# A 512-deep projection as seven block products instead of eight, in a hybrid streaming-encoder layer on one core

## The chip, the cores and the metric

The kernel runs on one core of a Trainium2 chip. The metric is the device time of one execution in microseconds (us). Five engines work from queues of their own: TensorE (PE, the matmuls), VectorE (DVE), ScalarE (ACT), GpSimd (POOL) and SyncE (SP, which only starts transfers). An instruction waits for the semaphores that it names, and what stands behind it on its engine waits with it.

## The reference, cut to what matters

One layer works on 1024 frames of 1024 features. Two mixers, a gated recurrence (`oa`) and a band attention (`ob`), each give 512 features for each frame; both are projected to 1024 features, gated and added, and the sum goes through the output projection. Then follow a SwiGLU and a gated embedding.

```python
h = rmsnorm(x, norm_mix_g[li])
z = h @ w_in[li]
qa, fa, ia, ga, qb, kb, vb, gate_a, gate_b = jnp.split(z, split_at, axis=-1)
oa = hgrn2_mixer(qa, fa, ia, ga, lower_bounds[li], hgrn_onorm_g[li])
ob = band_attention(qb, kb, vb, attn_qnorm_g[li], attn_knorm_g[li], attn_rel_bias[li])
merged = (jax.nn.sigmoid(gate_a) * (oa @ w_branch_a[li])
          + jax.nn.sigmoid(gate_b) * (ob @ w_branch_b[li]))
x = x + merged @ w_out[li]
h2 = rmsnorm(x, norm_ffn_g[li])
x = x + (jax.nn.silu(h2 @ w_ffn_gate[li]) * (h2 @ w_ffn_up[li])) @ w_ffn_down[li]
```

The change is about `ob @ w_branch_b` and what stands on both sides of it.

## The kernel before, in words

Everything is held with features on the 128 partitions and frames along the row. A float32 product is made of three matmuls on rounded operands: each operand is split into a rounded part (`hi`, written by ScalarE as a cast) and a residual (`lo`, source minus `hi`), and `gemm` (line 158) issues hi·hi, hi·lo, lo·hi. So every operand needs one cast on ScalarE and one subtraction on VectorE or GpSimd before TensorE can use it. Weights do the same: a unit of 128x1024 is loaded into one of two `raw` buffers, cast into `wh`, and its residual `wl` is written by GpSimd, or by VectorE and GpSimd by turns while `by_turns` is set (in the output projection). There are four buffers for `wh` and `wl` each. A raw buffer comes free when the residual is written, and the next load into it waits for that.

`order` (line 71) pins the order of the instructions on each engine as the program text issues them; VectorE, ScalarE and GpSimd calls through `self.V`, `self.A` and `self.G` are pinned too.

The stages that matter here, in order of time:

- The attention (`attention`, 32 steps of a pair of heads and 128 frames). `attn_pv` writes each result of 128 features by 128 frames to `ob[pair]`. The tiles of pairs 0 and 1 are stored to memory during the attention, those of 2 and 3 behind it, and all four are loaded again for the projection.
- The first branch (`branches`, first loop): 8 feature blocks by 2 halves of the frames, 12 matmuls of 128x512 each, the result times the gate into the tiles `m["B11"]` to `m["B22"]` (odd or even feature block, first or second half of the frames).
- The second branch (second loop): 8 by 2 results of 12 matmuls again, that is 192; VectorE multiplies each by its gate, and GpSimd (VectorE for the last four) adds it to the tile of `m`.
- The output projection (`out_proj`, through `passes`), a product of 2x2 blocks by the Winograd form of Strassen's method: seven products instead of eight, of sums of blocks of the weights and sums of blocks of `m`. Each pass is one product of 48 matmuls into four PSUM banks. The passes share three sets of banks; a later product adds onto an earlier one in the same bank. `added` adds each pass's banks into the residual stream `x`. The sums of `m` (T2, T3, T1, T4) are made by `branch_sums` on VectorE, for one half of the depth during the second branch and for the other at the start of the output projection, and `m_split` makes hi and lo of each operand. The sums of the weights (S1 to S4) are made in memory during the earlier stages by `dma_sums`: copies on SP's queue, then transfers with addition on POOL's queue.

In the text below, b: stands before a product of the second branch and o: before a pass of the output projection (o:A11 is the first one). Before the change the second branch has no such products.

Of the kernel before, what the change touches and what calls it, by code (L numbers as in the profile page):

```python
# [57 lines left out]
class Trunk:  # L58
# [334 lines left out]
    def hgrn_mix(self, h):  # L393
# [73 lines left out]
        for i in range(2):  # L467
# [4 lines left out]
            self.rest(False)  # L472
            yield 650
# [198 lines left out]
    def attn_pv(self, pair, b, pts, nb):  # L672
# [6 lines left out]
        self.last = self.A.copy(self.ob[pair][:, b * P:b * P + P], ps[:, :P])  # L679

    def attention(self):
# [41 lines left out]
        self.adds = chain(self.osum, self.wsum)  # L723
        for n in range(whole + 2):
# [4 lines left out]
            if n < whole:  # L729
                if steps[n][1] == 0:  # L730
                    self.ob.append(self.slot())
                scores(n, 0)
# [19 lines left out]
            if n == whole // 2 + 3:  # L752
                self.keep_heads(self.ob, self.obd, [0, 1])
# [234 lines left out]

    def branch_load(self, src):
# [7 lines left out]
    def branch_first(self):  # L997
        self.weights(0, ahead=3)
# [4 lines left out]
        for i, raw in enumerate(raws):  # L1003
            self.osrc.append(self.split(raw))
            yield
        self.keep_heads(self.ob, self.obd, [2, 3])
# [6 lines left out]
    def gate_load(self):  # L1013
        if len(self.bgates) < 2 * KC:
            for _ in range(2):
                t = self.slot(late=len(self.bgates) > 3)
                self.load(t, self.gd[len(self.bgates)])
                self.bgates.append(t)

    def branches(self):  # L1020
        nc, V = self.nc, self.V
        self.m = {}
        gates, load = self.bgates, self.gate_load
# [7 lines left out]
        src = self.osrc  # L1031
        for dd in range(4):
            (w,) = self.weights()
            next(self.adds, None)
            load()
            if dd == 1:
                raws = self.branch_load(self.obd)
                late = []
            for i in range(2):
                c = 2 * dd + i  # L1040
                for half in range(2):
                    hs = slice(half * HALF, half * HALF + HALF)
                    ps = yield from self.feature(w, src, half, off=i * HALF)
                    V.tensor_tensor(tile(c, half), ps, gates[c][:, hs], ALU.mult)
                    yield 2592
                if dd > 1:
                    late.append(self.split(raws[len(late)]))
        src = late
        for dd in range(4):
            (w,) = self.weights()  # L1050
            next(self.adds, None)
            load()
            for i in range(2):
                c = 2 * dd + i
                g = gates[KC + c]
                for half in range(2):
                    hs = slice(half * HALF, half * HALF + HALF)
                    ps = yield from self.feature(w, src, half, off=i * HALF)
                    V.tensor_tensor(g[:, hs], ps, g[:, hs], ALU.mult)
                    (self.G if dd < 3 else V).tensor_tensor(tile(c, half), tile(c, half), g[:, hs], ALU.add)  # L1060
                    yield 2592
            if dd == 1:
                self.branch_sums(0)
# [1141 lines left out]
```

## Time and profile before

| what | value |
|---|---|
| median of the runs | 1561.74 us (1558.86, 1561.74, 1562.02) |
| the profiled execution | 1560.97 us, its span 1559.2 us |
| granted TensorE clock, mean over the span | 0.999 |
| VectorE, ScalarE and GpSimd busy | 1126.4, 662.2 and 624.1 us |
| moved by transfers | 256.56 MB, mean 165 GB/s |

The span runs from the first to the last instruction; all positions below are microseconds from its start. A matmul's busy time overlaps the next one's, so TensorE's time in a stretch is read from the length of a stretch in which it does not wait, and not by adding up durations.

Stretches of the span, to find one's way: the attention ends at about 652, the first branch runs from there to 695.7, the second to 739.2, the output projection to about 817.

### The profile page before, as it was taken

How to read it: one execution, taken by the hardware profiler on the slowest of the kernel's cores; microseconds unless marked ns; L12 is line 12 of the kernel's file. 1: busy time of each engine (PE TensorE's matmuls, PEld its weight loads, DVE VectorE, ACT ScalarE, POOL GpSimd, SP SyncE). 2: the span in 40 equal slices, each digit the busy share in tenths (PEclk: the TensorE clock that was granted, in tenths of full speed). 3: DMA queues.
4: the chain of work that ended last, by engine and by line, in shares of the span. 5: the costliest groups of instructions: out<-in, count | busy, mean ns of one | idle time of the engine just before them, and what ended most of it. 6: DMA issues, size and time to landing. Idle time of an engine off the chain costs nothing.

```text
span 1559.2 us, 20881 instructions
## 1 busy us (share of the span) xinstructions
PE 1535.2 (98%) x7792; PEld 1281.2 (82%) x7792; DVE 1126.4 (72%) x1637; ACT 662.2 (42%) x1120; POOL 624.1 (40%) x349
## 2 busy tenths in 40 slices
PE   8999999999999999999999999999999999999998
PEld 6878888888888888788888888888888888888886
DVE  5777774676778778545988877777777766756667
ACT  6633333323367677521467322222222244446552
POOL 4243333010233222136211566665555545545546
PEclk9999999999999999999999999999999999999999
DMA  5453444887532343677344344443333288775325
GB/s 206 160 189 142 142 152 152 273 291 239 184 75 58 82 107 82 240 207 230 106 162 181 118 121 128 123 122 113 107 108 104 85 318 315 269 273 191 129 95 202
DMA packets 97094, 256.56 MB, mean 165 GB/s; under 512 B 10209, under 2 KB 14945, under 8 KB 96481
## 3 DMA queue, kind: packets, MB, share of 16 engines
q1 hardware_dynamic: 90448, 239.48, 44.1%
q0 software_dynamic: 6400, 15.73, 6.1%
q8 instruction: 61, 1.00, 0.3%
q14 instruction: 41, 0.33, 0.1%
q10 hardware_dynamic: 144, 0.02, 0.0%
HBM read 193.06 MB, written 93.59 MB: 184 GB/s over the span
## 4 chain that ended last, share of the span: by engine, by line
PE 91%; DVE 5%; DMA 2%; ACT 1%; issue 1%; SPq 0%; POOL 0%; DVEq 0%; ACTq 0%; POOLq 0%
PE pm L85 88%; DVE s L55 3%; PE pm L88 3%; DVE m L55 1%; DMA wr<-in_sz 0%; DVE q L55 0%; DMA wr<-in_su 0%; ACT m L55 0%; DMA s<-in_x 0%; DMA wr<-in_qk 0%; ACT wh L125 0%; SPq L80 0%; ACT s L55 0%; DVE s L227 0%; DVE wl L55 0%
## 5 line engine op out<-in xcount | busy, mean ns | idle before, releaser
L85 PE MATMUL pm<-s,whi 128*128 128x512 f32 x1792 | 551.7, 389 | 1.9 <-DVE t L55 1.9
L85 PE MATMUL pm<-s,wh 128*128 128x512 f32 (+1 forms) x1584 | 491.7, 391 | 7.5 <-ACT wh L125 5.0
L85 PEld LDWEIGHTS pm<-s,whi 128*128 128x128 f32 x1792 | 336.1, 188 | 72.3 <-DVE t L55 2.8
L85 PEld LDWEIGHTS pm<-s,wh 128*128 128x128 f32 x1584 | 295.3, 188 | 70.5 <-ACT wh L125 5.0
L85 PE MATMUL pm<-s,wlo 128*128 128x512 f32 x896 | 348.6, 389 | 0.0
L55 DVE TENSOR_TENSOR s<-s,s 128x512 f32<-128x512 f32 (+3 forms) x228 | 284.3, 1279 | 71.6 <-ACT s L55 42.7
L85 PE MATMUL pm<-s,wl 128*128 128x512 f32 x792 | 308.4, 389 | 0.5 <-POOL wl L133 0.5
L133 POOL TENSOR_TENSOR wl<-wr,wh 128x1024 fp32r<-128x1024 f32 (+2 forms) x72 | 175.6, 2443 | 220.5 <-ACT wh L125 207.2
L55 DVE TENSOR_TENSOR t<-pm,t 128x512 f32<-128x512 f32 x158 | 108.8, 689 | 128.9 <-PE pm L85 108.7
L85 PEld LDWEIGHTS pm<-s,wlo 128*128 128x128 f32 x896 | 168.2, 188 | 35.1
L125 ACT CAST wh<-wr 128x1024 fp32r<-128x1024 f32 (+2 forms) x106 | 106.5, 1005 | 208.9 <-PE pm L85 97.2
L85 PE MATMUL pm<-wh,s 128*128 128x512 f32 x512 | 179.9, 408 | 0.0
L85 PEld LDWEIGHTS pm<-s,wl 128*128 128x128 f32 x792 | 148.9, 188 | 31.9 <-POOL wl L133 1.2
L55 POOL TENSOR_TENSOR wlo<-wr,whi 128x512 fp32r<-128x512 f32 (+1 forms) x63 | 132.7, 2113 | 71.3 <-ACT whi L55 62.5
L55 POOL TENSOR_TENSOR wlo<-q,whi 128x512 fp32r<-128x512 f32 x62 | 97.2, 1568 | 139.7 <-ACT whi L55 110.6
L55 POOL TENSOR_TENSOR m<-m,mhalf 128x8 f32<-128x8 f32 (+1 forms) x24 | 35.0, 1458 | 241.3 <-DVE m L55 241.3
L55 ACT CAST whi<-q 128x512 fp32r<-128x512 f32 (+1 forms) x93 | 70.5, 759 | 110.6 <-PE pm L85 87.1
L55 ACT CAST s<-s 128x1024 fp32r<-128x1024 f32 (+1 forms) x94 | 90.4, 980 | 62.3 <-DVE s L55 31.8
L85 PEld LDWEIGHTS pm<-wh,s 128*128 128x128 f32 x512 | 96.9, 189 | 18.8
L55 POOL TENSOR_TENSOR s<-t,rb 128x512 f32<-128x512 f32 x44 | 70.7, 1608 | 99.3 <-ACT t L55 99.3
L85 PE MATMUL pm<-wl,s 128*128 128x512 f32 x256 | 100.5, 393 | 0.0
L55 ACT ACTIVATE t<-s 128x512 f32<-128x512 f32 x44 | 27.8, 632 | 158.3 <-DVE s L55 155.1
(145 smaller groups left out, 1850.0 us busy)
## 6 DMA issues: line engine op xcount, KB each, us to landing
s<-d SPq DMA_DIRECT2D x81, 512.0 KB, 6.3
d<-s SPq DMA_DIRECT2D x87, 256.0 KB, 2.3
wr<-d SPq DMA_DIRECT2D x36, 512.0 KB, 3.6
d<-s SPq DMA_DIRECT2D x32, 512.0 KB, 3.7
d<-t SPq DMA_DIRECT2D x46, 256.0 KB, 2.5
wr<-in_sg SPq DMA_DIRECT2D x22, 512.0 KB, 3.7
wr<-in_su SPq DMA_DIRECT2D x22, 512.0 KB, 4.1
s<-in_x SPq DMA_DIRECT2D x21, 512.0 KB, 8.2
```

The source lines that it names most:

```text
L55: return lambda *a, **k: self.trunk.order(op(*a, **k), self.key)
L85: return self.order(self.nc.tensor.matmul(*a, **k))
L88: return self.order(self.nc.tensor.transpose(*a, **k))
L125: self.nc.scalar.copy(hi[:, c], raw[:, c])
L133: rest.tensor_tensor(lo[:, c], raw[:, c], f32(hi[:, c]), ALU.subtract)
```

## The change

- The second branch becomes seven products of blocks. The attention's result is kept in SBUF in block layout: a tile for the odd or even pair of heads and each half of the frames (`ob[j, h]`, two pairs side by side). It is no longer stored and loaded again.
- `branch_ops` makes the sums and the hi and lo of these blocks on VectorE and ScalarE, partly during the first branch, partly during the second.
- The sums of the branch's weights are made by `dma_sums` in memory, as those of the output projection were: four copies and four adding transfers more. The adding transfers for the feed-forward weights come later in turn, eight more of them in the gate and up stage.
- `branch` runs the products kind by kind in the order A11, A12, S2, S1, S3, S4, A22, each 24 matmuls into four banks. After A11, S2 and S1 ScalarE copies the banks to SBUF, since a later product adds onto them or they are needed apart; after the others VectorE takes the copy off where needed, multiplies by the gate, and GpSimd (VectorE after A22) adds into `m`.
- The output projection runs its passes in the order `OUT_KINDS`: A12 second instead of third. After o:A11 and o:S2 ScalarE copies the banks, and VectorE adds them into `x` later from the copies. The sums of `m` for both halves of the depth are issued when o:A11's second operand has been taken, T1 and T4 when o:S2's have.

```diff
-        self.last = self.A.copy(self.ob[pair][:, b * P:b * P + P], ps[:, :P])
+        at = self.ob[pair % 2, b // 4]
+        at = at[:, pair // 2 * HALF + b % 4 * P:pair // 2 * HALF + b % 4 * P + P]
+        self.last = self.A.copy(at, ps[:, :P])
...
-        self.adds = chain(self.osum, self.wsum)
+        self.adds = chain(turns(self.bsum, self.osum), self.wsum)
...
-            if n == whole // 2 + 3:
-                self.keep_heads(self.ob, self.obd, [0, 1])
...
+    OUT_KINDS = (("A11", "B11"), ("A12", "B21"), ("S2", "T2"), ("S3", "T3"), ("S1", "T1"), ("A22", "T4"), ("S4", "B22"))
+    STEPS_B = (("A11", "y"), ("A12", "x"), ("S2", "y"), ("S1", "z"), ("S3", "y"), ("S4", "z"), ("A22", "y"))
...
+    def branch_split(self, src, sign=None, rest=None):
+        hi, lo = self.slot(F32R), self.slot(F32R)
+        if sign:
+            self.A.activation(hi, src, AF.Copy, scale=-1.0)
+            self.V.scalar_tensor_tensor(lo, src, -1.0, f32(hi[:, :]), ALU.mult, ALU.subtract)
+        else:
+            self.A.copy(hi, src)
+            (rest or self.V).tensor_tensor(lo, src, f32(hi[:, :]), ALU.subtract)
+        self.bready.append((hi, lo))
+
+    def branch_ops(self):
+        V, split = self.V, self.branch_split
+        b11, b12, b21, b22 = [self.ob[j, h] for j in range(2) for h in range(2)]
+        split(b11, -1)
+        yield
+        split(b21)
+        yield
+        V.tensor_tensor(b12, b12, b22, ALU.subtract)
+        V.tensor_tensor(b11, b11, b12, ALU.subtract)
+        yield
+        split(b11)
+        yield
+        t1 = self.slot()
+        V.tensor_tensor(t1, b11, b22, ALU.subtract)
+        split(t1)
+        yield
+        split(b12)
+        yield
+        split(b22)
+        yield
+        V.tensor_tensor(b21, b21, b11, ALU.subtract)
+        split(b21)
+        yield
...
     def branch_first(self):
-        self.weights(0, ahead=3)
         raws = self.branch_load(self.od)
...
-        self.keep_heads(self.ob, self.obd, [2, 3])
...
+    def branch(self, side):
...
+        def out(u, odd, half, src):
+            t = m[f"B{odd + 1}{half + 1}", u // 2][:, u % 2 * HALF:u % 2 * HALF + HALF]
+            g = gates[odd, half][u]
+            V.tensor_tensor(g, src, g, ALU.mult)
+            (V if (odd, half) == (1, 0) else G).tensor_tensor(t, t, g, ALU.add)
+
+        def after(kind, u, ps):
+            if kind in ("A11", "S2", "S1"):
+                A.copy(kept[kind][u], ps)
+            elif kind == "S3":
+                t = kept["S1"][u]
+                V.tensor_tensor(t, ps, t, ALU.subtract)
+                out(u, 1, 1, t)
+            elif kind == "A22":
+                out(u, 1, 0, ps)
+            else:
+                V.tensor_tensor(ps, ps, kept["A11" if kind == "A12" else "S2"][u], ALU.subtract)
+                out(u, 0, int(kind == "S4"), ps)
+
+        banks = {b: [self.mm() for _ in range(4)] for b in "xy"}
+        for kind, b in self.STEPS_B:
+            (w,) = self.weights(1)
+            hi, lo = self.bready.pop(0)
...
+            first, ps = kind in ("A11", "A12", "S1"), banks[b]
+            for j in range(2):
+                s = slice(j * HALF, j * HALF + HALF)
+                for u in range(4):
+                    c = slice(j * HALF + u * P, j * HALF + u * P + P)
+                    drain(self.gemm(
+                        ps[u], [(w[0][:, c], w[1][:, c], hi[:, s], lo[:, s])], first=first and j == 0, last=j == 1,
+                        **({} if first else {"skip_group_check": True})))
+                next(side, None)
+                yield 0
+            for u in range(4):
+                after(kind, u, ps[u])
+        drain(side)
...
+                    if half and dd + i > 1:
+                        next(self.bops)
...
+            for i in range(14):
+                if i in (1, 3, 5):
+                    next(self.bops)
+                if i in (2, 10):
+                    next(self.adds, None)
+                if i == 5:
+                    self.A.activation(self.warm, self.ones, AF.Silu)
+                if i in (7, 9):
+                    self.m_split()
...
-    def branch_sums(self, i):
+    def branch_sums(self, i, late=False):
         m, V = self.m, self.V
-        for kind in ("T2", "T1", "T4"):
-            m[kind, i] = self.slot()
+        if late:
+            for kind in ("T1", "T4"):
+                m[kind, i] = self.slot()
+            V.tensor_tensor(m["T1", i], m["T2", i], m["B22", i], ALU.subtract)
+            V.tensor_tensor(m["T4", i], m["B21", i], m["T2", i], ALU.subtract)
+            return
+        m["T2", i] = self.slot()
         V.tensor_tensor(m["B12", i], m["B12", i], m["B22", i], ALU.subtract)
         m["T3", i] = m["B12", i]
         V.tensor_tensor(m["T2", i], m["B11", i], m["T3", i], ALU.subtract)
-        V.tensor_tensor(m["T1", i], m["T2", i], m["B22", i], ALU.subtract)
-        V.tensor_tensor(m["T4", i], m["B21", i], m["T2", i], ALU.subtract)
...
             got = ready.pop(0)
             if len(ready) < 2:
                 split()
+            if (b, i) == ("B11", 1):
+                self.branch_sums(0)
+                self.branch_sums(1)
+            if b == "T2":
+                self.branch_sums(i, True)
             return got
...
+        def after(kind, u, ps):
+            if kind in ("A11", "S2"):
+                self.A.copy(p1[u], ps)
+                todo.append((kind, u, p1[u]))
+            else:
+                added(kind, u, ps)
+
+        def side():
+            for _ in self.ffn_side():
+                if todo:
+                    added(*todo.pop(0))
+                yield
+
+        yield from self.passes(4, operand, after, side(), kinds=self.OUT_KINDS)
...
-                self.copies = chain(islice(self.osum, 8), islice(self.wsum, 4 * STEPS))
+                self.bsum = self.dma_sums(d["bq"], 2, self.bsums)
+                self.copies = chain(islice(self.bsum, 4), islice(self.osum, 8), islice(self.wsum, 4 * STEPS))
```

How the built program stands, engine by engine, at the three places that the prediction speaks of. In these rows `pm` is a PSUM bank, `wr`, `wh`, `wl` a weight raw, rounded and residual, `s` any tile in SBUF; the number behind a name tells one tile from another.

VectorE from the last operand of the second branch to the first banks of b:S3, after the change:

```order
L55 TENSOR_TENSOR s_3947<-s_3947,s_3891 128x1024
L55 TENSOR_TENSOR s_7031<-s_3947,s_7030 128x1024
L55 TENSOR_TENSOR s_7076<-s_6627,s_7075 128x1024
L55 TENSOR_TENSOR s_7128<-s_6764,s_7127 128x1024
L55 TENSOR_TENSOR s_7049<-pm_6894,s_7049 128x512
L55 TENSOR_TENSOR s_6999<-s_7049,s_6999 128x512
L55 TENSOR_TENSOR s_7049<-pm_6895,s_7049 128x512
L55 TENSOR_TENSOR s_6999<-s_7049,s_6999 128x512
```

The first two rows are b:A22's operand (b21 less b11, and its residual); the next two are the residuals of m's two B11 tiles, for o:A11; behind them stand the banks of b:S3 (`pm_6894` and the next three). Before the change nothing but a multiplication by the gate stood behind a result of the second branch.

GpSimd from the last adds of b:S3's results to the weights of the output projection's third pass, after the change:

```order
L55 TENSOR_TENSOR s_6813<-s_6813,s_7000 128x512 x2
L55 TENSOR_TENSOR wl_7147<-wr_7149,wh_7148 128x1024
L55 DMA d_3159<-d_3132 128x1024
L55 TENSOR_TENSOR s_6642<-s_6642,s_7093 128x512 x2
L55 TENSOR_TENSOR s_6779<-s_6779,s_7094 128x512 x2
L55 TENSOR_TENSOR wl_7200<-wr_7202,wh_7201 128x1024
L133 TENSOR_TENSOR wl_7285<-wr_7287,wh_7286 128x1024
L133 TENSOR_TENSOR wl_7369<-wr_7371,wh_7370 128x1024
```

The two `x2` rows in the middle are the adds of b:S4's four results, and right behind them stand the residuals of both units of o:A12's weights (`wl_7200`, `wl_7285`). Before, the residuals of the output projection's first weights alternated with adds in the same way, but the last four results of the branch were added on VectorE with no add left on GpSimd.

ScalarE where the copies of o:A11's banks stand, after the change:

```order
L55 CAST s_7291<-s_6798 128x1024
L55 COPY s_7251<-pm_7253 128x512
L55 COPY s_7251<-pm_7254 128x512
L125 CAST wh_7330<-wr_7331 128x1024
L55 COPY s_7252<-pm_7255 128x512
L55 COPY s_7252<-pm_7256 128x512
```

The first row is the cast of m's second B21 tile; the copies are those of o:A11's four banks, onto which o:A12 adds, and between them stands the cast of o:S2's first weights (`wh_7330`), which waits for a load. Before, no copy from PSUM stood on ScalarE in this stage.

134 lines of the change are left out of this document (76 added, 58 removed).

## The prediction

> **What bounds the kernel now.** I read the page's busy shares first, then the chain that ended last in order of time, then what TensorE waited for between 612 and 900, then the stretches.
>
> ```profile
> PE 1535.2 (98%) x7792; PEld 1281.2 (82%) x7792; DVE 1126.4 (72%) x1637; ACT 662.2 (42%) x1120; POOL 624.1 (40%) x349
> ...
> 641.33 97.86 PE pm L85 x460
> ...
> 749.69 1.22 DVE s L55
> 750.96 94.25 PE pm L85 x423
> ...
> PE pm L88 <- DVE m L55: 2.8, 1, 2.8
> PE pm L85 <- DVE s L55: 0.7, 1, 0.7
> ...
> 652.10:695.70 43.60, 43.60 (x193) 36.06 (x193) 18.07 (x23) 10.64 (x12) 13.69 (x8) 1.00 0.83 261
> 695.70:739.20 43.50, 43.50 (x193) 36.04 (x192) 21.90 (x24) 6.09 (x7) 29.56 (x20) 1.00 0.71 221
> 739.20:816.80 77.60, 76.91 (x339) 63.36 (x338) 68.20 (x76) 44.77 (x55) 16.29 (x6) 1.00 0.44 141
> ```
>
> TensorE is never idle from 641.3 to 739, so a matmul taken out there is worth its pitch; around the place there are two waits, 2.8 us ahead of it and 0.7 us at about 750. The columns of a stretch are its length, then the busy times of TensorE, its weight loads, VectorE, ScalarE and GpSimd, the clock and the transfers. The second branch is the stretch from 695.7: 43.5 us for 192 matmuls, a pitch of 0.2266 us. Three matmuls take 0.68 us, a block product of 24 takes 5.44, a pass of 48 takes 10.88. VectorE has 21.90 us of work in these 43.5, but 68.20 in the 77.6 of the output projection behind it. There the change has no room to spend.
>
> **What it takes away.** 24 matmuls: 24 x 0.2266 = 5.4 us. The wait of 0.7 at 750 stands in an order of passes that no longer exists, so it goes. The 2.8 us have a cause that the change moves.
>
> ```profile
> 634.94 2.36 POOL L55 TENSOR_TENSOR wl<-wr,wh 128x1024 fp32r<-128x1024 f32 x1 [22.06 <-ACT wh L125]
> ...
> 635.01 2.84 DVE L55 TENSOR_TENSOR wl<-wr,wh 128x512 fp32r<-128x512 f32 x1
> ...
> 637.96 0.55 DVE L55 TENSOR_SCALAR m<-m,m 128x640 f32<-128x640 f32 x1
> ...
> 638.66 0.74 PE L88 MATMUL pm<-eye,m 128*128 128x128 f32 x5 [2.75 <-DVE m L55]
> ```
>
> VectorE's residual of 512 columns took 2.84 us: it ended 0.55 behind GpSimd's residual. The softmax scaling at 637.96 stood behind it, and TensorE's transposes behind that. The weights that GpSimd worked on there were asked for by the line that the change drops from branch_first; in the changed program their cast stands behind the last scaling on ScalarE. With 0.6 us in place of 2.84 this wait falls by 2.2 us (from 0, if GpSimd collides with something there all the same, to 2.75). Gains: 5.4 + 0.7 + 2.2 = 8.3 us.
>
> The 4 stores and 4 loads of the attention's tiles that go away, the four added copies and four added transfers, and the 8 adding transfers that move to the gate and up stage I cost at nothing: TensorE waited for none of them, and GpSimd is held about 1.1 us by one, with 3.5 us idle behind it. If that cover were gone it would be 8 x 1.1 = 9 us, in the third rival's direction.
>
> ```profile
> 915.26 1.10 POOL L55 DMA_DIRECT2D d<-in_wq  x1
> 919.91 1.28 POOL L55 TENSOR_TENSOR wlo<-q,whi 128x512 fp32r<-128x512 f32 x1 [3.54 <-ACT whi L55]
> ```
>
> **What it adds.** First a rule of the queues, read from pairs of rows.
>
> ```profile
> 679.97 1.22 DVE L214 TENSOR_TENSOR s<-s,s 128x1024 fp32r<-128x1024 f32 x1
> ...
> 685.76 2.41 POOL L55 TENSOR_TENSOR wl<-wr,wh 128x1024 fp32r<-128x1024 f32 x1 [7.52 <-ACT wh L125]
> 686.66 2.60 DVE L214 TENSOR_TENSOR s<-s,s 128x1024 fp32r<-128x1024 f32 x1 [1.16 <-ACT s L213]
> ...
> 696.63 2.40 POOL L55 TENSOR_TENSOR wl<-wr,wh 128x1024 fp32r<-128x1024 f32 x1 [7.45 <-ACT wh L125]
> 698.40 0.69 DVE L55 TENSOR_TENSOR s<-pm,s 128x512 f32<-128x512 f32 x1 [2.03 <-PE pm L85]
> ...
> 743.95 8.10 DVE L55 TENSOR_TENSOR s<-s,s 128x1024 f32<-128x1024 f32 x5
> 745.65 3.04 POOL L133 TENSOR_TENSOR wl<-wr,wh 128x1024 fp32r<-128x1024 f32 x1 [7.44 <-ACT wh L125]
> ```
>
> A VectorE operation with both sources in SBUF takes 1.22 alone, but 2.60 when GpSimd is at work: it ends one own duration behind GpSimd's (685.76 + 2.41 + 1.1). One that reads PSUM keeps its 0.69 beside GpSimd. In the last pair five such operations took 8.10 instead of 5.7, 2.4 more, one GpSimd operation; GpSimd lost 0.6 itself, and got in between two of VectorE's. So they take turns, each waiting for the other's whole operation. [...]
>
> The other durations:
>
> ```profile
> 731.04 0.69 DVE L55 TENSOR_TENSOR s<-pm,s 128x512 f32<-128x512 f32 x1
> 731.77 0.85 DVE L55 TENSOR_TENSOR s<-s,s 128x512 f32<-128x512 f32 x1
> ...
> 751.96 7.25 DVE L55 TENSOR_TENSOR s<-s,pm 128x512 f32<-128x512 f32 x12
> ...
> 704.62 1.29 POOL L55 TENSOR_TENSOR s<-s,s 128x512 f32<-128x512 f32 x1 [1.43 <-DVE s L55]
> ...
> 824.12 1.55 ACT L55 COPY s<-pm 128x512 f32<-128x512 f32 x3
> ...
> 653.95 1.28 ACT L55 ACT_TABLE_LOAD   x1
> ...
> 647.65 3.88 ACT L213 CAST s<-s 128x1024 fp32r<-128x1024 f32 x4
> ...
> wr<-d SPq DMA_DIRECT2D x36, 512.0 KB, 3.6
> ```
>
> An operation that uses the result of the one ahead starts 0.73 behind it (731.04 to 731.77), an independent one 0.61 (7.25 / 12). So a subtraction and a multiplication on one bank take 1.34. A residual or sum of 1024 is 1.15 in a row, GpSimd's add 1.3 and residual 2.4, a ScalarE copy 0.53 and cast 0.97 in a row, a weight's load 3.6.
>
> Now the clock from 695.7, where the second branch starts. If TensorE never waited, b:S3 would end at 722.9, b:A22 start at 728.3, the output projection at 733.8, o:A12 at 744.6, o:S2 at 755.5, o:S3 at 766.4.
>
> Up to b:S3: b:A11's last bank is done at 701.1. ScalarE then copies, casts a weight and casts b22 until 703.8; its residual waits for GpSimd's weight until 704.6 and ends at 705.75. Four pairs for b:A12 end at 711.1, b21's sum at 712.3. ScalarE follows with a cast, the table load, four copies of b:S2, a weight, a cast, four copies of b:S1 and another weight, until 722.0, and casts m's second B11 tile until 723.0. All copies are in time for TensorE (b:S3 has 0.6 us to spare or more). But the weight's cast at 722.0 starts GpSimd's residual, to 724.4, a moment before VectorE's residual of B11 can start; this ends at 725.6. b:S3's banks, ready from 720.9, stand behind it.
>
> - b:A22 adds onto b:S3's banks. Each pair there ends with an operation in SBUF that waits for GpSimd's add (0.65 + 1.3): the fourth subtraction ends at 731.6, wanted at 728.3 + 3 x 0.68 = 730.35. Wait **1.3** (0 without the collisions, 3 with one residual more ahead).
> - o:A11 takes over b:S4's banks. Their four pairs run from 732.9 to 738.3; o:A11, from 735.1, wants the fourth at 737.15. Wait **1.1** (0 to 1.2).
> - o:A12 starts at 747.2 by now. Its operand needs the last of four results of b:A22, multiplied and added on VectorE from 738.3. GpSimd has b:S4's adds and two weights' residuals at the same time: from 738.7 on 3 x 1.3 + 2 x 2.4 = 8.7 us of it, and VectorE's 4 x 0.65 + 1.15 = 3.75 in SBUF, in turns: 751.2. Wait **4.0**. Even if VectorE wins each turn, the copies of o:A11's last two banks stand behind a cast whose weight loads only when the residual of the one before is done (at about 745, + 3.6 + 1.0 + 0.5 = 750.1, wanted 748.6): 1.5 is the lower bound, 4.5 the upper.
> - o:S2, from 762.1: 6 sums and residuals and a weight, 8 us, just end in time; the second operand stands behind six adds and meets one GpSimd residual: wait **1.3** (0 to 2.4).
> - o:S3, nominally 774.3 by now: its operand stands behind six more adds, four PSUM adds, a weight: 769.1 + 3.7 + 2.5 + 2.3 = 777.5. Wait **3.2** (0 to 3.5).
>
> Sum of waits: 1.3 + 1.1 + 4.0 + 1.3 + 3.2 = 10.9 us (1.5 to 14.6). Behind o:S3 VectorE catches up: in each later pass it had room before.
>
> ```profile
> 770.79 2.73 DVE L55 TENSOR_TENSOR s<-s,pm 128x512 f32<-128x512 f32 x4 [1.47 <-PE pm L85]
> ...
> 781.67 2.73 DVE L55 TENSOR_TENSOR s<-s,pm 128x512 f32<-128x512 f32 x4 [2.03 <-PE pm L85]
> ```
>
> T1 and T4 of both halves come on top there, 4.6 us over two passes with 1.5 to 2 idle each; I take nothing for it, at most 1.
>
> **The sum.** -8.3 + 10.9 = +2.6 us, on the profiled execution's own 1560.97: 1563.6. The median of the runs lies 0.8 above that execution, so I say 1564.0, 2.3 above 1561.74.
>
> **The rivals.**
>
> First, the waits are covered, and the matmuls are gained. Without any collision VectorE is in time everywhere: from b:S3's evacuation to o:S3's operand it has 38.8 us of work (12 pairs at 1.35, and 22.6 of sums, residuals and adds), from 724.3 to 763.1, and TensorE wants that operand at 766.4. For it speaks the group's mean, little above 1.22:
>
> ```profile
> L55 DVE TENSOR_TENSOR s<-s,s 128x1024 fp32r<-128x1024 f32 x18 | 22.5, 1268 | 0.9 <-ACT s L55 0.9
> ```
>
> Against it: that is a stretch where GpSimd had 16.29 us of work in 77.6. It decides if the collisions cost under a third of what I count. Time: 1561.7 - 8.3 + 0 to 5 = 1553.4 to 1558.4, say 1555.
>
> Second, half of the collisions: 1561.7 - 8.3 + 5 to 9 = 1558.4 to 1562.4, no change. It needs VectorE to win the turns at o:A12 and o:S3.
>
> Third, slower beyond doubt: o:A12 and what follows it hang on weights' loads. The cast of o:S2's first weights stands on ScalarE ahead of o:A11's last two copies; its load starts when GpSimd has finished the unit before, which itself stands behind four adds. If such a load takes 6.3 us (what tiles take here in the median) instead of 3.6, o:A12 and o:S2 each lose 2.7 more, and the eight transfers moved to the gate and up stage may add a little: 1564 + 5.4 = 1569. It decides as soon as GpSimd's residual for o:A12 ends later than about 747. Against it: few other transfers run there, 0.44 of the engines.
>
> ```profile
> s<-d SPq DMA_DIRECT2D x81, 512.0 KB, 6.3
> ```
>
> **Chances.** My forecast, 1562.4 to 1566.5, has 0.45, about half of it within 0.2% of 1561.74; the first rival 0.28, the second 0.12, the third 0.15. A measurement of this kernel tells about 0.2%, 3.1 us, from no change. So faster 0.29 (the first rival and a sliver of the second), same 0.31 (most of the second and under half of the forecast), slower 0.40. The range 1554 to 1569 holds the forecast, the second rival and most of the other two; the forecast's own is 1562 to 1567.
>
> **What would show it.** In the changed profile: TensorE's wait at about 636 under 1 us; TensorE waiting for VectorE at about 728 to 731, at 735 to 738, and most of all near 747 (all of these some 2 us earlier, by what the attention's tail gains); VectorE's residuals there 2 to 3.6 us long, beside GpSimd's; VectorE without idle time from about 724 to 777. The prediction is wrong if TensorE runs through from 641 to 817 without a wait, or if it waits elsewhere: for ScalarE's copies in the second branch, or for a weight's load.

## The result, and the profile after

| | before | changed |
|---|---|---|
| median of the runs | 1561.88 us (4 runs, 1558.86 to 1563.69) | 1572.43 us (4 runs, 1570.59 to 1574.65) |
| the profiled execution, its span | 1560.97 us, 1559.2 us | 1574.65 us, 1572.9 us |
| granted TensorE clock, mean over the span | 0.999 | 0.992 |

The ratio is 1.0067 (95% interval 1.0053 to 1.0081). The change makes the kernel 10.5 us slower. The prediction was 1564.0 with 1554 to 1569 as its range, so the result lies outside. The sign of the likeliest case was right, the size was not.

First the busy times over the whole span of the changed kernel, from its page, and what TensorE waited for between 612 and 900 us (total, times, longest):

```profile
PE 1538.1 (98%) x7768; PEld 1281.0 (81%) x7768; DVE 1157.1 (74%) x1655; ACT 678.0 (43%) x1146; POOL 650.6 (41%) x357
```

```profile
PE pm L85 <- ACT whi L55: 4.8, 1, 4.8
PE pm L85 <- ACT s L55: 3.5, 1, 3.5
PE pm L85 <- DVE s L55: 2.0, 4, 0.9
PE pm L85 <- DVE t L55: 1.9, 1, 1.9
...
PE pm L88 <- DVE m L55: 0.6, 1, 0.6
```

24 matmul records are gone (7792 before), yet TensorE is busy 2.9 us longer: some of what is left ran slower. The two largest waits are for ScalarE, and before the change TensorE never waited for it here. The waits stand in TensorE's timeline (start, duration, instruction, idle time ahead of it and its releaser):

```profile
728.30 0.73 PE L85 MATMUL pm<-s,wh 128*128 128x512 f32 x2 [0.45 <-DVE s L55]
...
743.70 0.39 PE L85 MATMUL pm<-s,wl 128*128 128x512 f32 x1
747.56 0.80 PE L85 MATMUL pm<-s,wh 128*128 128x512 f32 x1 [3.48 <-ACT s L55]
749.28 0.79 PE L85 MATMUL pm<-s,wh 128*128 128x512 f32 x1 [0.93 <-DVE s L55]
...
750.30 1.05 PE L85 MATMUL pm<-s,wh 128*128 128x512 f32 x2
...
756.59 0.62 PE L85 MATMUL pm<-s,wh 128*128 128x512 f32 x2
...
818.39 0.50 PE L85 MATMUL pm<-ph,wl 128*128 128x512 f32 x1 [1.14 <-DVE wl L133]
825.78 1.22 PE L85 MATMUL pm<-s,whi 128*128 128x512 f32 x2 [4.79 <-ACT whi L55]
827.92 0.79 PE L85 MATMUL pm<-s,wlo 128*128 128x512 f32 x1 [0.93 <-DVE wlo L55]
```

In order of place: b:A22 (728.3; two short ones of o:A11 at 733.6 and 734.9 are left out), o:A12 (747.6 and 749.3), the embedding and the first product of the gate and up stage (818 to 828). Two matmuls take 1.05 us behind the wait of o:A12, and 0.62 six us later. The stretches of the profile show why (length, busy time of TensorE, its weight loads, VectorE, ScalarE, GpSimd, then the granted clock and the transfers):

```profile
743.20:746.60 3.40, 0.88 (x4) 0.38 (x3) 3.33 (x6) 2.62 (x3) 1.21 (x1) 1.00 0.20 75
746.60:753.40 6.80, 4.91 (x11) 3.54 (x12) 6.76 (x5) 4.96 (x8) 2.27 (x2) 0.50 0.24 77
753.40:756.80 3.40, 3.40 (x16) 2.78 (x15) 3.40 (x2) 0.45 (x1) 2.75 (x1) 0.99 0.00 0
...
825.10:831.90 6.80, 5.20 (x11) 3.64 (x12) 6.32 (x7) 2.23 (x5) 0.00 (x0) 0.50 0.05 18
...
879.70:883.10 3.40, 1.46 (x7) 1.05 (x6) 1.97 (x2) 1.92 (x4) 3.40 (x4) 1.00 0.46 154
883.10:886.60 3.50, 3.50 (x10) 2.73 (x9) 3.47 (x3) 1.33 (x2) 3.28 (x2) 0.51 0.00 0
```

Behind each stretch of 3.4 us in which TensorE was idle for more than half of the time (busy 0.88 us at 743.2 and 1.46 at 879.7; the one at 821.7, idle throughout, is left out), its clock is at half. A long wait is paid twice here: once as the wait, and once as slow matmuls after it.

The balance is made from the starts of TensorE's matmuls in both profiled executions: every distance from one start to the next, less the pitch of 0.2266 us. A wait comes out some 0.15 longer this way than the idle time in the brackets above.

| where | us |
|---|---|
| 24 matmuls fewer | -5.4 |
| wait at the attention's tail, 2.9 to 0.8 | -2.2 |
| wait at 750 before, gone | -0.9 |
| b:A22 and o:A11 | +1.9 |
| o:A12: the wait, and the half clock behind it | +5.1 and +2.1 |
| embedding and first gate and up product: waits, and half clock | +7.7 and +2.1 |
| the wait at 879 (870 before), 0.9 to 2.1, and half clock | +1.2 and +1.6 |
| sum | +13.2 |

The spans differ by 13.7. So the gains came as predicted, and the loss came from two places: 9.1 us up to o:A12, and 12.6 behind the output projection.

What held o:A12 up is seen in VectorE's and GpSimd's timelines.

```profile
735.51 6.45 DVE L55 TENSOR_TENSOR s<-s,s 128x512 f32<-128x512 f32 x1
```

```profile
733.80 5.26 POOL L55 TENSOR_TENSOR s<-s,s 128x512 f32<-128x512 f32 x4
738.79 2.61 POOL L55 TENSOR_TENSOR wl<-wr,wh 128x1024 fp32r<-128x1024 f32 x1
```

VectorE's first add of b:A22, worth 0.7 us, lasts 6.45. It starts while GpSimd is at its second add, and ends only when GpSimd's fourth add and the residual behind it are through (738.79 + 2.61 = 741.40, and 0.6 for the add itself). VectorE got no turn in between: it waited out the rest of one add, two more adds and a residual.

The same happens the other way round 40 us later, and this starts the late stall. First VectorE, GpSimd, then the queue of transfers (SP) and ScalarE:

```profile
778.13 1.22 DVE L133 TENSOR_TENSOR wl<-wr,wh 128x1024 fp32r<-128x1024 f32 x1
...
781.60 4.16 DVE L55 TENSOR_TENSOR s<-s,s 128x512 f32<-128x512 f32 x5
785.68 2.48 DVE L55 TENSOR_TENSOR s<-s,pm 128x512 f32<-128x512 f32 x4
```

```profile
777.28 10.76 POOL L133 TENSOR_TENSOR wl<-wr,wh 128x1024 fp32r<-128x1024 f32 x1 [7.13 <-ACT wh L125]
792.81 2.40 POOL L133 TENSOR_TENSOR wl<-wr,wh 128x1024 fp32r<-128x1024 f32 x1 [4.77 <-PE pm L85]
```

```profile
779.38 9.03 SPq L80 DMA_DIRECT2D wr<-in_ow  x2
795.24 0.33 SPq L80 DMA_DIRECT2D wr<-d  x1
795.62 1.85 SPq L80 DMA_DIRECT2D s<-in_p  x4
```

```profile
791.68 1.05 ACT L125 CAST wh<-wr 128x1024 fp32r<-128x1024 f32 x1 [4.63 <-DMA wr<-in_ow]
...
802.42 1.05 ACT L55 CAST ph<-s 128x1024 fp32r<-128x1024 f32 x1 [0.29 <-DMA s<-in_p]
```

GpSimd's weight residual of 2.4 us lasts 10.76; in the kernel before, its five residuals of this stage last 2.42 to 3.25. It gets its 2.4 us from 785.64 on, just when VectorE turns from SBUF operands to its four adds that read PSUM (785.68). Then everything behind it is late in turn: the second load of in_ow goes out when that residual frees its buffer (788.1), lands for ScalarE's cast at 791.68, GpSimd's next residual ends at 795.2, the load behind that one goes out at 795.24, and the four loads of in_p, which stand behind it on SP's queue, at 795.62. ScalarE, on which the program pins the order, casts ph at 802.42; in the kernel before it did so by 792.9 (at 790.88, 1.99 us for both). All that ScalarE has for the next stage stands behind this cast.

From 808.6 on, the chain of work that led to the late waits runs mostly over VectorE, and two of its operations there wait out a GpSimd residual (2.58 and 3.42 in place of 1.22):

```profile
808.63 2.58 DVE L55 TENSOR_TENSOR s<-s,s 128x1024 fp32r<-128x1024 f32 x1 [2.15 <-ACT s L55]
...
814.91 3.42 DVE L133 TENSOR_TENSOR wl<-wr,wh 128x1024 fp32r<-128x1024 f32 x1
```

So the late stall has at least three shut-outs in it, one of GpSimd and two of VectorE. How much each of them costs was not measured apart.

### The profile page after: what moved, and what is told of

It reads as the page before. It is cut to its first block, busy times and chain, and to the rows that moved or that the text cites. A ratio compares the mean times of both kernels' runs of the same rounds, so it can differ in the third digit from the quotient of the medians.

```text
span 1572.9 us, 20899 instructions
## 1 busy us (share of the span) xinstructions
PE 1538.1 (98%) x7768; PEld 1281.0 (81%) x7768; DVE 1157.1 (74%) x1655; ACT 678.0 (43%) x1146; POOL 650.6 (41%) x357
## 4 chain that ended last, share of the span: by engine, by line
PE 88%; DVE 6%; DMA 2%; ACT 2%; issue 2%; POOL 0%; SPq 0%; DVEq 0%; ACTq 0%; POOLq 0%
PE pm L85 86%; DVE s L55 3%; PE pm L88 3%; DVE m L55 1%; ACT s L55 1%; DMA wr<-in_su 0%; DVE q L55 0%; DMA wr<-in_sz 0%; ACT m L55 0%; DMA s<-in_x 0%; ACT wh L125 0%; DMA s<-in_p 0%; DMA wr<-in_qk 0%; SPq L80 0%; DVE pm L55 0%
## 5 line engine op out<-in xcount | busy, mean ns | idle before, releaser
L85 PE MATMUL pm<-s,wh 128*128 128x512 f32 x1568 | 489.0, 393 | 11.7 <-ACT wh L125 5.0
L55 DVE TENSOR_TENSOR s<-s,s 128x512 f32<-128x512 f32 (+3 forms) x258 | 323.5, 1289 | 78.7 <-ACT s L55 50.8
L85 PE MATMUL pm<-s,wl 128*128 128x512 f32 (+1 forms) x784 | 306.2, 391 | 0.5 <-POOL wl L133 0.5
L133 POOL TENSOR_TENSOR wl<-wr,wh 128x1024 fp32r<-128x1024 f32 (+3 forms) x73 | 191.1, 2621 | 214.3 <-ACT wh L125 205.2
L125 ACT CAST wh<-wr 128x1024 fp32r<-128x1024 f32 (+3 forms) x109 | 109.7, 1007 | 194.2 <-PE pm L85 69.4
L55 ACT CAST s<-s 128x1024 fp32r<-128x1024 f32 (+1 forms) x100 | 97.0, 986 | 69.3 <-DVE s L55 44.2
L55 POOL TENSOR_TENSOR wl<-wr,wh 128x1024 fp32r<-128x1024 f32 x23 | 58.2, 2531 | 95.1 <-ACT wh L125 81.4
```

The lines of the kernel that those rows point to most:

```text
L55: return lambda *a, **k: self.trunk.order(op(*a, **k), self.key)
L85: return self.order(self.nc.tensor.matmul(*a, **k))
L125: self.nc.scalar.copy(hi[:, c], raw[:, c])
L133: rest.tensor_tensor(lo[:, c], raw[:, c], f32(hi[:, c]), ALU.subtract)
```

## The experiments

Two theories were set against each other. **A**: VectorE and GpSimd shut each other out of SBUF, each for as long as the other's row of instructions goes on, and the waits follow from single shut-outs. **B**: VectorE has too much work for the time from 724 to 810, as the prediction had it, and moving one piece only moves the wait. All kernels were run against the kernel before on the same chip, and that had medians of 1561.62 to 1561.94 in the four sets.

| kernel | median us (runs) | ratio to before, 95% | mean clock of its runs |
|---|---|---|---|
| before | 1561.6 to 1561.9 (85) | | 0.9973 |
| changed | 1572.43 (4) | 1.0067 (1.0053 to 1.0081) | 0.9928 |
| e1_psum_add | 1568.80 (6) | 1.0054 (1.0037 to 1.0070) | 0.9948 |
| e2_embed_first | 1569.28 (5) | 1.0046 (1.0032 to 1.0059) | 0.9942 |
| e3_residuals_on_dve | 1566.47 (12) | 1.0025 (1.0015 to 1.0036) | 0.9949 |
| e4_tail_alone | 1557.80 (10) | 0.9978 (0.9970 to 0.9987) | 0.9987 |
| e5_both | 1559.83 (12) | 0.9991 (0.9982 to 1.0000) | 0.9971 |
| e6_second_adds | 1563.05 (12) | 1.0011 (1.0001 to 1.0022) | 0.9957 |
| e7_before_tail_dve | 1556.88 (5) | 0.9970 (0.9958 to 0.9982) | 0.9990 |
| e8_one_long_wait | 1562.33 (12) | 1.0004 (0.9991 to 1.0016) | 0.9972 |
| e9_four_short_waits | 1560.80 (12) | 0.9995 (0.9984 to 1.0006) | 0.9978 |
| e10_last_turns | 1563.45 (12) | 1.0011 (1.0002 to 1.0019) | 0.9951 |

### e1: one shut-out taken away

```diff
-            V.tensor_tensor(g, src, g, ALU.mult)
-            (V if (odd, half) == (1, 0) else G).tensor_tensor(t, t, g, ALU.add)
+            if (odd, half) == (1, 0):
+                V.tensor_tensor(src, src, g, ALU.mult)
+                V.tensor_tensor(t, t, src, ALU.add)
+                return
+            V.tensor_tensor(g, src, g, ALU.mult)
+            G.tensor_tensor(t, t, g, ALU.add)
```

> The changed kernel, with b:A22's product left in its PSUM bank, so that the four adds of VectorE behind it read PSUM and not two SBUF tiles; the same number of VectorE instructions. Theory A (VectorE is shut out of SBUF by GpSimd's whole row of back-to-back instructions, 735.5 to 741.4): that add takes 0.7 us instead of 6.45, o:A12's operand is ready some 5 us earlier, TensorE's wait ahead of o:A12 falls from 5.1 us to under 1.5, its clock stays at full speed there (another 2 us), and the whole is 5 to 7 us shorter, 1565 to 1568. Theory B (VectorE has too much work of its own there, the shut-out is a side show): the time is taken by the residuals and sums behind, and under 2 us are gained, 1570 to 1573.

VectorE's timeline at the first of the four adds and at the instructions behind the last, then TensorE ahead of o:A12:

```profile
733.46 0.69 DVE L55 TENSOR_TENSOR s<-s,pm 128x512 f32<-128x512 f32 x1
...
738.06 7.01 DVE L55 TENSOR_TENSOR s<-s,s 128x1024 fp32r<-128x1024 f32 x3
```

```profile
742.86 0.50 PE L85 MATMUL pm<-s,wh 128*128 128x512 f32 x1 [0.58 <-DVE s L55]
```

The add takes 0.69 in place of 6.45, while GpSimd goes through the same row of work. TensorE waits 0.6 us in place of 3.48 + 0.93, and the clock stays full there. That is theory A, with the number of VectorE's instructions unchanged. What came of it in time is not clear: the profiled execution is 7.3 us shorter (span 1565.6), the median 3.6, which falls between the two theories' ranges, and by the ratios it is 2 (1.0067 to 1.0054, the intervals overlap). Waits of 1.0 us at o:S3 and 0.9 in o:S4 appear, which were not there while TensorE came 7 us later, and the late stall stands as it was (4.8 us for ScalarE).

### e2: the loads that came late, one place earlier

```diff
                     self.ffn_rest(kind, i)
+                    if i:
+                        raws = [self.embed_raw(h) for h in range(2)]
...
-                self.embed_load(0, True)
-                self.embed_load(1, False)
+                self.embed_cast(raws.pop(0), True)
+                self.embed_cast(raws.pop(0), False)
```

> The changed kernel, with the four loads of in_p one step earlier on SP's queue: ahead of the weight load that waits for GpSimd's residual of 792.8 to 795.2, behind the one that waits for the residual ending at 788.0. Nothing else is changed in the loads. Theory A (the late stall of 1.3 + 5.0 + 1.3 us and the slow clock behind it hang on these loads, which hang on the freed weight buffer): the casts of ph start near 793 instead of 801 to 802.4, TensorE's waits between 816 and 828 fall under 2 us, no half-speed clock there, 7 to 9 us shorter, 1563 to 1566. Theory B (VectorE and ScalarE are late by their own work): the waits stay over 5 us, and the time within 2 us of 1572.4.

The loads of in_p went out at 787.4, ScalarE cast ph at 794.4, both as meant, and the wait of 1.14 us in the embedding was gone. But the wait for whi was still 3.3 us, and the time 3.1 us shorter by the medians (the intervals overlap), not 7 to 9. The chain of waits of this kernel names the rest:

```profile
776.16 10.84 POOL wl L133
787.02 3.44 DMA wr<-in_ow
```

It starts at the same residual of GpSimd, 10.8 us long. So the order of the loads was one link, and the shut-out residual stands ahead of it. That the loads alone did it, as I had expected, is wrong.

### e3: no weight residual on GpSimd

```diff
-        rest = self.nc.vector if self.by_turns and self.turn % 2 else self.G if ...
+        rest = self.nc.vector if self.by_turns else self.G if ...
```

> The changed kernel, with every weight residual of the output projection on VectorE, none on GpSimd (7 more VectorE instructions of 1.15 us, 8 us). Theory A (the two engines shut each other out): no GpSimd residual lasts 7 to 11 us there any more, the weight buffers come free earlier and with them the loads of in_p; the late stall falls by more than half, while the wait ahead of o:A12, whose GpSimd work is the second branch's adds, shrinks little; 1564 to 1570. Theory B (VectorE has too much work): 8 us more work on it lengthen the waits, 1574 to 1580.

With 8 us more work on VectorE the kernel is 6 us faster than the changed one. What TensorE waited for from 612 to 900 is down to this (two more are under 0.7 us):

```profile
PE pm L85 <- ACT s L55: 3.5, 1, 3.5
PE pm L85 <- DVE wlo L55: 1.4, 1, 1.4
PE pm L85 <- DVE s L55: 1.0, 3, 0.5
```

The wait for whi is gone, the one ahead of o:A12 (3.5) is what it was. Theory B would have made both longer. With e1 it shows that the two places have two causes of one kind. The edit takes more away than the shut-outs, since a residual takes VectorE 1.15 us and GpSimd 2.4 even alone; but of the 10.76 us only 2.4 were GpSimd's own work.

### e5, e6: both edits, and one more

e5_both has the edits of e1 and e3 together.

> The changed kernel with both edits of e1_psum_add and e3_residuals_on_dve: b:A22's adds read PSUM, and all residuals of the output projection are on VectorE. Theory A (each edit removes its own shut-out): the wait of 5.1 us ahead of o:A12 and its slow clock go as in e1, the late stall goes as in e3, and what is left of waits is b:A22 and o:A11 (1.9 us), some 1.5 ahead of the gate and up stage and up to 2 of VectorE's work: 1559 to 1562, which is under the kernel before or equal to it. Theory B (VectorE's time is what is short, and an edit only moves the wait): more VectorE work with less time for it, no better than e3 alone, 1565 to 1568.

The waits went as in e1 and in e3, and the time is 1559.83, 12.6 us under the changed kernel: more than the 10.5 that the change had cost (the edit of e3 by itself, without the change, is worth 0.9 by the medians of e4 and e7 below, whose intervals overlap). In e6_second_adds the products of b:S4 stay in PSUM too, and VectorE adds them:

```diff
-            if (odd, half) == (1, 0):
+            if (odd, half) in ((1, 0), (0, 1)):
```

> e5_both, and b:S4's four products and adds too are left in PSUM and done by VectorE (four more VectorE instructions, 2.4 us; four GpSimd instructions of 1.3 less). Theory A: GpSimd's row of six back-to-back instructions at 731.8 to 741.7 becomes two, VectorE's residual behind it (7.0 us for three instructions in e1) is shut out for one residual at most, and the time is 1 to 3 us under e5. Theory B: VectorE has 2.4 us more to do ahead of o:A12, TensorE's wait there grows by about that, 1 to 3 us over e5.

It is 3 us slower than e5, as theory B had it. But the wait grows not at o:A12, where none is left, but at o:A11, which takes over b:S4's banks. VectorE and TensorE there:

```profile
730.15 1.43 DVE L55 TENSOR_TENSOR pm<-pm,s 128x512 f32<-128x512 f32 x2
...
732.22 1.43 DVE L55 TENSOR_TENSOR pm<-pm,s 128x512 f32<-128x512 f32 x2
```

```profile
734.42 0.74 PE L85 MATMUL pm<-s,wh 128*128 128x512 f32 x2 [1.10 <-DVE s L55]
...
736.49 0.95 PE L85 MATMUL pm<-s,wh 128*128 128x512 f32 x2 [1.10 <-DVE s L55]
```

A bank now takes VectorE 2.07 us (730.15 to 732.22) in place of 1.33, and TensorE needs one every 0.68. Already two instructions a bank are slower than TensorE, as the prediction's terms for b:A22 and o:A11 had it, and a third makes the wait at o:A11 grow from 0.6 to 3.2 us. A stretch of 3.4 us at half clock follows (736.8). The 3 us of the medians are not explained by this alone: the profiled execution of e6 is its fastest (1559.76), and its waits from 612 to 900 add up to 6.6 us, as e5's do (6.7), because others are shorter there.

### e10: the last residuals back on GpSimd

In e5 VectorE has no idle time from 765 to 809, and two waits of 0.6 and 1.4 us follow. e10_last_turns gives GpSimd three of the seven residuals back that e3 had taken from it, late ones.

```diff
-        rest = self.nc.vector if self.by_turns else ...
+        rest = self.nc.vector if self.by_turns and (self.all_v or self.turn % 2) else ...
...
+            if b == "T1":
+                self.all_v = False
```

> e5_both, with the residuals of the last two passes of the output projection and of the embedding taken in turns with GpSimd again (three of 1.15 us off VectorE, from some 787 on). In e5 VectorE has no idle time from 765 to 809, and TensorE then waits 0.8 + 1.6 us for what comes off it at 812 to 815. Theory B at this place (VectorE's own work is what is late there): these two waits fall under 1 us together, 1.5 us faster than e5, 1558 to 1559. Theory A (shut-outs): GpSimd's residuals there are held up by VectorE's rows again, to 5 us and more, the loads behind them come late, and it is 1 to 5 us slower than e5.

It is slower than e5, 1563.45 to 1559.83: theory A again. GpSimd, the queue of transfers and TensorE:

```profile
796.08 5.03 POOL L133 TENSOR_TENSOR wl<-wr,wh 128x1024 fp32r<-128x1024 f32 x1 [12.39 <-ACT wh L125]
```

```profile
793.12 8.35 SPq L80 DMA_DIRECT2D wr<-in_pp  x2
```

```profile
814.84 0.73 PE L85 MATMUL pm<-s,whi 128*128 128x512 f32 x2 [2.79 <-ACT whi L55]
```

One residual lasts 5.03 again, the second load of in_pp goes out when it has ended (801.1), and the wait for whi is 2.8 us, in place of e5's 0.6. Another of the three met VectorE's adds that read PSUM and lasted 2.41. 3.45 us less work on VectorE bought nothing.

### e4, e7: the tail alone, and the fastest

```diff
     def branch_first(self):
-        self.weights(0, ahead=3)
```

> The kernel before, with only the call in branch_first dropped that asks for the first branch's weights three units ahead. If the wait of 2.8 us at 636 to 638 was VectorE's residual held up by GpSimd's work for that call, it falls to about 0.6 and the time from 1561.9 to 1559.7. If the weight then comes too late for the first branch, TensorE waits there instead and the time is 1561 to 1564.

TensorE waited 0.59 us at the tail (2.75 before), and nowhere in the first branch. The time is 3.9 us under the kernel before, more than the 2.2 of the wait; the section on the hardware says where the rest may lie. e7_before_tail_dve adds the edit of e3 to this, without the change.

> The kernel before, with the tail edit of e4_tail_alone and with all residuals of the output projection on VectorE: what the edit of e3 is worth without the change. TensorE waits for nothing there in e4 (0.7 us at 748 aside), so theory A expects 1557 to 1559, equal to e4; if the residuals on GpSimd cost something elsewhere, it is faster than 1556; if VectorE has no room for 8 us more work, slower than 1560.

1556.88 is the fastest of all, 5 us under the kernel before. From e4 it can't be told (the intervals overlap). e5 is the changed kernel on the same footing (it has e1's edit besides), and 3 us slower than e7 by the medians: the 24 matmuls are worth 5.4 us, but TensorE waits 6.7 us between 612 and 900 in e5 and 1.5 in e7, and 3.4 us at half clock (868.5) come on top in e5.

### e8, e9: what a wait costs

Both build on e7. In the first branch VectorE rewrites an operand tile with its own values, in e8 four times in a row (`4 * (dd == 1)`), in e9 once behind each weight unit (`1`).

```diff
+                    if (i, half) == (0, 1):
+                        for _ in range(4 * (dd == 1)):
+                            hold = src[0][0]
+                            V.tensor_tensor(hold, f32(hold[:, :]), f32(hold[:, :]), ALU.max)
                     V.tensor_tensor(tile(c, half), ps, gates[c][:, hs], ALU.mult)
```

> e7_before_tail_dve, with four VectorE instructions of 1.15 us in a row that rewrite an operand tile of the first branch with its own values, between two of its products: one wait of TensorE of about 4.8 us, in a place where it has none. If a wait costs its length, 4.8 us more than e7 (1561 to 1562.5, even with the kernel before). If TensorE's clock falls to half for a window of 3.4 us behind a window that was over half idle, as it seems in the changed kernel, 1.5 to 2.5 us more: 1563 to 1564.5, and the clock of the profile has a half-speed stretch right there.

> The same four VectorE instructions, one behind each weight unit of the first branch, 11 us apart: four waits of about 1.3 us, 5.2 in all, more than in e8. If a wait costs its length, 1562 to 1563, 0.4 slower than e8. If it is the half-idle window that takes the clock down, none of these waits does it, the clock stays full there, and the time is 1562 to 1563 but 1 to 2 us under e8.

The waits came out shorter than planned, one of 3.1 us in e8, two of 1.2 and 0.8 in e9, so the times expected for them decide nothing. The stretches of e8, then of e9, around them:

```profile
668.80:672.20 3.40, 0.99 (x4) 0.85 (x5) 2.92 (x3) 0.00 (x0) 0.00 (x0) 1.00 1.05 334
672.20:675.60 3.40, 3.40 (x9) 2.66 (x9) 0.00 (x0) 0.00 (x0) 1.08 (x1) 0.50 1.02 417
675.60:679.00 3.40, 3.40 (x16) 2.76 (x15) 1.08 (x2) 0.61 (x1) 0.00 (x0) 0.99 1.09 313
```

```profile
674.40:677.80 3.40, 2.23 (x11) 1.54 (x9) 3.40 (x3) 0.65 (x1) 2.17 (x1) 1.00 0.99 219
677.80:681.20 3.40, 3.40 (x15) 2.83 (x16) 2.03 (x3) 0.00 (x0) 1.06 (x1) 1.00 0.48 160
```

Behind the long wait 9 matmuls ran in 3.4 us, and 16 in the next 3.4; behind the short one the clock stayed. That shows the half clock behind a long wait at a place where only the wait was put in. Its price in the medians stays open: by the ratios e8 lies 5.3 us over e7 and e9 3.9, each with an interval of some 2 us, and each more than its waits.

## Why the prediction was wrong

By its own steps (the sum as it stands there, 10.9 less 8.3 on 1561.74, gives 1564.3 and not 1564.0):

- **24 matmuls, 5.4 us; the wait at 750, 0.7; the tail, 2.2.** Right. The balance has 5.4, 0.9 and 2.2, and e4 shows the cause of the third by itself.
- **b:A22 1.3 and o:A11 1.1.** Right in the mechanism, 0.7 and 1.2 measured; in e6 the same step, with one instruction a bank more, gave three waits of 1.0 to 1.1 at o:A11.
- **o:A12 4.0, at most 4.5.** The wait is there and is the first large one, but 5.1 long, with 2.1 of half clock behind it. The rule it was worked out by, "they take turns, each waiting for the other's whole operation", failed: VectorE waited out two whole adds and a residual of GpSimd's in a row, besides the rest of the add that was at work. e1 shows that this shut-out, and not the sum of VectorE's work, made the wait. The lower bound of 1.5, from ScalarE's copies behind a cast, was too high: 0.8 is left there in e5, for ScalarE, and 0.6 in e1.
- **o:S2 1.3 and o:S3 3.2.** Neither came in the changed kernel, where TensorE was 7 us late by o:A12. With that wait gone, in e1, TensorE waits 1.0 at o:S3 and nowhere in o:S2. Both were too large.
- **"Behind o:S3 VectorE catches up", nothing, at most 1.** This is the step that failed: 9.8 us were lost there, waits and clock, more than the whole error of 8.4. I asked only whether VectorE had time, and it had: it stood idle four times between 791 and 811. What was late was GpSimd, shut out by VectorE's own unbroken row (the deferred adds and T1's and T4's sums among it), and through it a weight buffer, two loads, the loads of in_p and ScalarE's queue. e3 takes GpSimd's residuals away, and of the waits of 6.9 us there 1.4 are left; e10 brings three residuals back to e5, and the wait for ScalarE grows by 2.2.
- **The third rival** named weight loads behind GpSimd's residual, and 1569. Its mechanism is the one at work, but it put it at o:A12 and o:S2, where loads cost nothing, and not at the end. That TensorE "waits elsewhere", for ScalarE's copies in the second branch or for a weight's load, was given as the sign of a wrong prediction, and it is close to what its waits show behind the second branch: 3.5 and 4.8 us for ScalarE.
- **The clock** had no term at all. 5.8 us of the balance are matmuls at half speed behind waits.
- **The second rival**, half of the collisions and 1558.4 to 1562.4, is where e5 lies with its 1559.8, but only after two edits. The first rival, waits covered and 1555, was reached by none of the changed kernels' medians.
- **The transfers moved to the gate and up stage, at nothing.** Not tested alone. The wait at 879 (1.9 us for VectorE's t) has 1.9 in e2 and e5 too, 0.3 to 0.65 in e1, e6 and e10, and none in e3, which all have these transfers. A weight's load (in_su) that stands ahead of it in the chain took 6.40 us before the change and 7.45 after, but 7.58 and 7.72 in e1 and e10, where the wait is short. What decides it stays open.

## What to carry to other kernels

Where VectorE and GpSimd both work on SBUF, look for unbroken rows of instructions and not at busy shares: an instruction of one engine can wait for the rest of the other's row (6.45 us in place of 0.7 and 10.76 in place of 2.4 in the changed kernel), and what costs is all that stands in order behind it, on either engine, down to a load whose buffer comes free late. Leaving a product in PSUM, so that the add behind it reads PSUM, cost VectorE no time in e1 (0.69 us for such an add, 0.69 for one with both sources in SBUF that met nothing, at 742.60 in the changed kernel) and took it out of the contest; where TensorE already waits for the banks, as in e6, more work on them costs (the waits at o:A11 grew from 0.6 to 3.2 us). Moving work to the idler engine can be the wrong way: e10 is 3.6 us slower than e5. Waits of some 1.9 us and more within 3.4 us were followed by half clock here (2.1 us more behind o:A12) and have to be priced with it, whether it is one wait or, as in e6, three short ones.

## What the runs showed of the hardware

**An engine can be kept out over a row of the other's.** The traces show a VectorE add with both sources in SBUF waiting while GpSimd is at work, and one that reads PSUM not (6.45 us in the changed kernel, 0.69 in its place in e1). They show that the wait can be longer than one instruction: VectorE waited for the rest of one GpSimd add, two more adds and a residual (6.45 us), and GpSimd for nine VectorE instructions that started after it had (10.76 us in place of 2.4). Seven GpSimd residuals between 600 and 830 us took 5 us or more: 6.97 and 10.76 in the changed kernel, 7.75 and 11.01 in e1, 7.03 and 10.83 in e2, 5.03 in e10. In the changed kernel the last 2.4 us of both begin when VectorE goes on to operands in PSUM (767.75 and 785.64, against 767.79 and 785.68), those of e1's first too (761.30 against 761.36), and those of e10's when VectorE pauses for 0.36 us (798.7 against 798.84). But a row does not always win. Here GpSimd got in behind the first of VectorE's six instructions, and lost only 0.35 us:

```profile
745.25 8.65 DVE L55 TENSOR_TENSOR s<-s,s 128x512 f32<-128x512 f32 x6
```

```profile
745.39 2.75 POOL L133 TENSOR_TENSOR wl<-wr,wh 128x1024 fp32r<-128x1024 f32 x1 [3.99 <-ACT wh L125]
```

The pair at 743.95 and 745.65 that the prediction read its turns from is such a case too (GpSimd's residual 3.04 in place of 2.4). What decides who comes next is not shown.

**The clock fell behind stretches that were over half idle.** The half-speed stretches last 3.41 or 6.83 us and lie on a fixed grid of 3.41 us (in the changed kernel they begin at 94.67, 746.61, 825.12 and 883.15, which are 191, 23 and 17 such lengths apart). In the twelve profiles, from 25 to 1540 us, all 17 stretches of the grid at full clock with 1.88 us of idle time or more (55%) were followed by half speed, among them 2.03 at 510.6 before the change and 2.25, 2.53, 3.41 and 1.94 at 91.3, 743.2, 821.7 and 879.7 after it. Of the eight with 1.55 to 1.81 us one was (1.55, in e3 at 817.3), and of all others only one place, near 848, in five of the profiles, where TensorE spends 1.84 us on 16 matmuls of a single column and counts as busy. The tail stretch:

```profile
636.80:640.30 3.50, 1.64 (x10) 1.50 (x11) 2.10 (x4) 0.48 (x1) 0.50 (x1) 1.00 0.03 11
640.30:643.70 3.40, 3.40 (x34) 2.73 (x34) 0.42 (x1) 0.48 (x1) 0.00 (x0) 1.00 0.00 0
```

TensorE was busy 1.64 of 3.5 us there and kept its clock; with 1.46 of 3.4, at 879.7 in the changed kernel, it lost it. So it matters how a wait falls on the grid. At about 513 us TensorE waits in all twelve profiles. Before the change two waits of 1.73 and 0.31 us lay in one stretch, and half speed followed (from 513.97); after it the first, 1.57, lay in one stretch and the 0.31 in the next, and the clock stayed. In e4 the 1.58 us, with 0.31 of the next wait, lay in one stretch, and half speed followed; in e8 2.66 us were divided over two stretches (1.50 and 1.47 idle), and the clock stayed. One and the same wait can cost more in some executions than in others. The runs fit this. Over the 85 runs of the kernel before, the mean granted clock and the span go together (correlation -0.86, 1.16 us for each 0.001 of clock). e4's runs have 0.0014 more clock than before's, 1.6 us, and with the 2.2 of the wait this makes 3.8 of the 3.9 that e4 gained. The changed kernel's runs have 0.0045 less, 5.2 us by the same slope, half of what it lost.
